# Encoder layer (HGRN2 and neighbourhood attention): keys and queries of the first attention half as seven block products in a stretch of their own

## The chip, the cores and the metric

The kernel runs on one core of one Trainium2 chip. The metric is the time of one execution on the device in microseconds (us), the median of several runs; lower is better. Five engines take part, each with its own instruction queue: PE (TensorE, matrix products), DVE (VectorE), ACT (ScalarE), POOL (GpSimd) and SP (SyncE, which only issues DMAs here). PE writes its results to PSUM banks; ACT and DVE move them from there to SBUF.

## What is computed

One layer over 2048 tokens (a grid of 32 rows by 64 columns) of width 1024, all in float32:

```python
h = layernorm(x) * (1 + scale) + shift          # scale, shift, gate from c @ ada_w
q_h, i_h, zf_fw, zf_bw, g_h, q_n, k_n, v_n, g_n = split(h @ w_in)   # 9 x 1024 columns
y_hg = hgrn2(q_h, i_h, zf_fw, zf_bw, g_h)       # gated linear recurrence, two directions, 8 heads
o_na = neighbourhood_attention(q_n, k_n, v_n, rpb)   # 16 heads of 64, 8 x 16 window of the grid
y = concat([y_hg, o_na * silu(g_n)]) @ w_out
out = layernorm(2**0.25 * x + gate * y) * ln_g + ln_b
```

## The kernel before

**Numbers.** A float32 matrix is multiplied as a sum of a rounded part (`hi`, type float32r) and the rest (`lo`): `hi*hi + hi*lo + lo*hi`, three matmuls for one product of a 128x128 block of weights with 128x512 of h (`proj_mm`, L278 to 282). A split of a 128x512 tile is one ACT copy (`hi`) and one DVE subtraction (`lo`).

**h.** h is kept transposed as tiles `hts[g, k, s]`: token group g (512 tokens each), feature block k (8 of 128), s = 0 for `hi` and 1 for `lo`. Only one half of the tokens (1024, two groups) is on chip at a time.

**Order of the whole.** PE's order is the program's; DVE, ACT, POOL and SP get theirs from a scheduler that orders instructions by readiness and priority, except where an instruction is `pinned` to its place in the program. The stages are: start-up (layer norm of the first half, h, and unit 0's projections); the first attention half; HGRN over 8 heads and two halves; the second attention half; the output projection. A "unit" is a pair of attention heads (128 columns of each of keys, queries and gate; values go by two units, 256 columns).

**Start-up** (`startup`). Besides unit 0's keys, queries and gate it multiplies values of units 0 and 1 (`vproj`) and, in one place, the first group of unit 1's keys (`fourth`, L1294 to 1313).

**First attention half** (`first_half`). Eight units of four tiles each (`natten_woven`): scores (4 matmuls, L1067 and L1074), bias addition and softmax on DVE and ACT (L1083 to L1093), transposes on PE (L1116), copies to SBUF (L1120, L1122), and one step later the sums with the values (L1138). While the tiles of unit u run, PE also works through a "dense" stream: `first_stream` of unit u+1, that is every second time a value block, and then keys, queries and gate, 2 groups x 8 k x 3 matmuls each (`NCOL0` gives the columns). The last unit runs beside the projections of the first HGRN head (`hgrn_dense`). `weave` hands out the dense work in equal shares, two for each tile (`yield` in `natten_woven`), with `KUS` = 0.68 us counted for three matmuls. Weights come through `Chunks`: a 128x512 tile is loaded by SP's queue, split, and freed; four tiles each of raw, `hi` and `lo`.

**Preparation of a unit** (`Prep`). `piece` is called as soon as a projection group is in SBUF: `k` copies the two heads' keys to `KA` and `KB` (L1002), moves each copy to the other 64 partitions by a DMA from SBUF to SBUF (L1003; SP's queue in the first half, POOL's in the second), and writes the rest to `KL` (L1004); `q` and `gate` are alike. What the second attention half will need again is stored to DRAM (`nq_d`, `nk_d`, `ng_d`). `table` loads the position bias for a tile; `v` loads value tiles from DRAM.

**Beside it.** `first_half` also carries the rest of the modulation's gate vector (`gate_load`, `gate_sum`), the bias tables' writing to DRAM (`bias_pair`), and the layer norm of the second half of the tokens, whose transposed h is stored to DRAM (`rows`, `stats`, `scale`, `piece`).

**Pools.** Tags that a stage shares with others go to common buffers (`SH`: "e" 8, "q" 4, "vt" 4, "gt" 2, "sg" 4, "bk" 4 tiles of 128x512); a stage's own tags stand in `NB0` and the like, and a mapping (`SM0`) says which of its names use the common ones. PSUM: 2 banks "pj" for dense work, and 2 each of "sc", "pt" and "po".

**Output projection.** It already takes two token tiles at a time as seven block products (`OutPair`, matmuls at L1672 to L1674), with sums of y made on DVE and splits on POOL (L1656).

Of the kernel before, what the change touches and what calls it, by code (L numbers as in the profile page):

```python
# [10 lines left out]
F32 = mybir.dt.float32  # L11
# [27 lines left out]
def body(ctx: ExitStack, tc: tile.TileContext, t):  # L39
# [38 lines left out]
    nq_d = [dram(f"nq{i}", (P, 512)) for i in range(NPAIR)]  # L78
    nk_d = [dram(f"nk{i}", (P, 768)) for i in range(NPAIR)]
# [670 lines left out]
    def load_bias(p, j, kind, pin=lambda x: x):  # L750
# [5 lines left out]
        elif kind == "top":  # L756
            dma(bf[0:64, 0:11 * 64], table_ap(tint[p], 22, jt, 4, 4, 11))
            dma(bf[64:128, 0:8 * 64], table_ap(tedge[p], 15, jt, 4, 4, 8))
# [114 lines left out]
    def first_srcs():  # L873

        r = [t["w_v"][0][:, i * 512:(i + 1) * 512] for i in range(4)]
        for u in range(1, 8):
            if u % 2 == 0:
                r += [t["w_v"][u // 2][:, i * 512:(i + 1) * 512] for i in range(4)]
            r += [t["w_in"][c // P + u][:, i * 512:(i + 1) * 512] for _, c in NCOL0 for i in range(2)]
        return r + [t["w_in"][c // P][:, i * 512:(i + 1) * 512] for _, c in HCOL for i in range(2)]  # L880

    def first_stream(st, feed):

        if st.p % 2 == 0:
            for _ in vproj(t["w_v"][st.p // 2], nv_d[st.p // 2], 0, feed):
                feed.tick()
                yield 2.9
        todo = []
        for n, c in NCOL0:
            his, los = feed.take(2)  # L890
            for g in range(2):
                if st.raws[n][g]:
                    todo = [(n, g)]
                    continue
                pz = ps("pj")
                for k in range(KT):
                    proj_mm(pz, his, los, g, k)
                    if k == KT - 1:
                        st.raws[n][g] = evac(pz)
                        todo = [(n, g)]  # L900
                    if g == 1 and k % 4 == 3:
                        feed.free()
                    feed.tick()
                    if k == 1 and todo:
                        st.piece(*todo.pop())
                    yield KUS
        st.piece(*todo.pop())
# [52 lines left out]
    class Prep:  # L960


        def __init__(self, p, half, raws):
            self.p, self.half, self.raws = p, half, raws
            self.first = half and p == 0
            self.keep = half and p in (0, 7)
            self.Q, self.V, self.sg, self.bias, self.bk = {}, {}, {}, {}, {}

        def fetch(self, name):
            store, n0, n1 = {"q": (nq_d, 0, 512), "g": (ng_d, 0, 512), "k0": (nk_d, 0, 512), "k1": (nk_d, 512, 768)}[name]  # L970
            raw = tl("bk")
            dma(raw[:, 0:n1 - n0], store[self.p][:, n0:n1])
            self.bk[name] = raw

# [1004 lines left out]
```

## Time and profile before

| | us |
|---|---|
| median of 3 runs | 2556.86 (2555.92 to 2558.54) |
| profiled execution | 2557.55 |
| its span, first to last instruction | 2555.7 |
| PE busy in the span | 2531.9 |
| DVE busy | 1807.0 |
| ACT busy | 1487.8 |
| POOL busy | 260.5 |
| start-up, until the first dense matmul of the first attention half | 91.9 |
| first attention half, to about | 517 |
| granted TensorE clock | 0.999 of full speed |

A matmul's busy time in the profile overlaps that of the next one, since they are pipelined; distances from start to start tell what one costs PE. "PEld" is the loading of a matmul's weights, which runs beside the matmul before.

### The profile page before, as it was taken

Reading aid. Unit: us, or ns where it says so; the run is one execution under the profiler, and the core shown is the slowest. Engines: PE = TensorE matmul, PEld = TensorE weight load, DVE = VectorE, ACT = ScalarE, POOL = GpSimd, SP = SyncE. Lnnn points to the kernel's source line nnn. Section 1 sums busy time; section 2 is a strip of 40 time slices with the busy share of each in tenths; the row PEclk is TensorE's granted clock in tenths of the full one; section 3 lists DMA queues with packets and bytes.
Section 4 is the critical chain, followed back from the end, with each engine's and each line's share of the span. In section 5 each row is a group of like instructions: output and inputs, shape, how many; then the busy total and the mean of one; then the engine's idle time right before and its main releaser. Section 6 shows DMA issues by size and latency. Waiting matters only on the chain.

```text
span 2555.7 us, 46330 instructions
## 1 busy us (share of the span) xinstructions
PE 2531.9 (99%) x17124; PEld 2142.6 (84%) x17124; DVE 1807.0 (71%) x4479; ACT 1487.8 (58%) x2968; POOL 260.5 (10%) x361
## 2 busy tenths in 40 slices
PE   8999999999999999999999999999999999999998
PEld 7888888888888888888888888999888888888887
DVE  7545545387877778868887887646777778867776
ACT  5533544376666666666666666545677768752331
POOL 0000000000000000000000000011122222224442
PEclk9999999999999999999999999999999999999999
DMA  7576454212122226222222222445566667664552
GB/s 297 144 210 156 143 173 148 94 51 71 67 75 71 71 71 224 99 79 85 62 70 82 85 83 83 134 117 150 129 136 145 140 140 167 178 207 132 162 168 99
DMA packets 227202, 319.55 MB, mean 125 GB/s; under 512 B 37159, under 2 KB 110503, under 8 KB 225831
## 3 DMA queue, kind: packets, MB, share of 16 engines
q1 hardware_dynamic: 210175, 278.51, 35.7%
q0 software_dynamic: 16800, 38.07, 6.4%
q8 instruction: 135, 2.21, 0.4%
q14 instruction: 92, 0.75, 0.1%
HBM read 233.90 MB, written 74.33 MB: 121 GB/s over the span
## 4 chain that ended last, share of the span: by engine, by line
PE 94%; DVE 3%; DMA 2%; ACT 1%; issue 1%; SPq 0%; POOL 0%; DVEq 0%; ACTq 0%; POOLq 0%
PE pj L282 53%; PE pj L295 7%; PE ps L1138 4%; PE ps L1674 3%; PE ps L1672 3%; PE ps L1673 3%; PE ps L1116 3%; PE ps L488 2%; PE ps L480 2%; PE ps L1067 2%; PE ps L555 1%; PE ps L1072 1%; PE ps L584 1%; PE ps L586 1%; PE ps L527 1%; PE ps L667 1%
## 5 line engine op out<-in xcount | busy, mean ns | idle before, releaser
L282 PE MATMUL pj<-h,wh 128*128 128x512 f32 x3984 | 1265.0, 399 | 0.2 <-ACT vt L303 0.2
L282 PEld LDWEIGHTS pj<-h,wh 128*128 128x128 f32 x3984 | 721.6, 188 | 148.7 <-issue 10.5
L282 PE MATMUL pj<-h,wl 128*128 128x512 f32 x1992 | 780.2, 392 | 0.0
L282 PEld LDWEIGHTS pj<-h,wl 128*128 128x128 f32 x1992 | 373.8, 188 | 81.8
L1088 ACT ACTIVATE pbuf<-pbuf,mx 128x480 f32<-128x480 f32 (+5 forms) x256 | 152.4, 596 | 90.5 <-DVE mx L1083 89.8
L295 PE MATMUL pj<-wh,h 128*128 128x256 f32 x1024 | 195.0, 285 | 0.3 <-ACT e L797 0.3
L1083 DVE CUSTOM_DVE_ANT_1 pbuf<-ps,bias 128x480 f32<-128x480 f32 (+5 forms) x256 | 129.1, 539 | 80.8 <-PE ps L1072 62.1
L295 PEld LDWEIGHTS pj<-wh,h 128*128 128x128 f32 x1024 | 162.9, 191 | 3.5 <-issue 0.9
L273 DVE TENSOR_TENSOR wl<-wr,wh 128x512 fp32r<-128x512 f32 x192 | 131.2, 684 | 44.2 <-ACT wh L272 43.9
L272 ACT ACTIVATE wh<-wr 128x512 fp32r<-128x512 f32 x192 | 120.2, 626 | 70.8 <-PE pj L282 64.3
L295 PE MATMUL pj<-wl,h 128*128 128x256 f32 x512 | 144.7, 283 | 0.0
L1122 ACT ACTIVATE pt<-ps 120x384 f32<-120x384 f32 (+3 forms) x128 | 65.2, 509 | 125.8 <-PE ps L1116 125.7
L1656 POOL TENSOR_TENSOR yl<-yr,yh 128x512 fp32r<-128x512 f32 (+1 forms) x80 | 109.6, 1380 | 147.0 <-ACT yh L1655 121.9
L1120 DVE COPY pt<-ps 120x384 f32<-120x384 f32 (+3 forms) x128 | 74.8, 584 | 63.1 <-PE ps L1116 62.1
L1116 PE MATMUL ps<-ident,pbuf 128*128 128x128 f32 (+2 forms) x832 | 112.6, 272 | 0.8 <-ACT Z L789 0.2
L1116 PEld LDWEIGHTS ps<-ident,pbuf 128*128 128x128 f32 (+2 forms) x832 | 96.6, 136 | 18.3 <-DVE pbuf L1093 1.9
L1655 ACT ACTIVATE yh<-yr 128x512 fp32r<-128x512 f32 (+1 forms) x80 | 47.9, 607 | 102.2 <-DMA yr<-yq 39.5
L474 DVE TENSOR_TENSOR de<-e,de 128x512 f32<-128x512 f32 x64 | 44.2, 691 | 88.2 <-ACT de L473 88.2
L797 ACT ACTIVATE e<-pj 128x512 f32<-128x512 f32 x96 | 57.3, 597 | 83.9 <-PE pj L282 75.9
L1093 DVE TENSOR_SCALAR pbuf<-pbuf,mx 128x480 f32<-128x480 f32 (+5 forms) x256 | 99.9, 411 | 3.3
L295 PEld LDWEIGHTS pj<-wl,h 128*128 128x128 f32 x512 | 97.9, 191 | 1.0
L849 DVE TENSOR_TENSOR wl<-wr,wh 128x512 fp32r<-128x512 f32 x68 | 46.8, 690 | 66.8 <-ACT wh L848 64.5
(361 smaller groups left out, 4897.8 us busy)
## 6 DMA issues: line engine op xcount, KB each, us to landing
wr<-in_w_in SPq DMA_DIRECT2D x276, 256.0 KB
yr<-yq SPq DMA_DIRECT2D x78, 256.0 KB
bias<-tint POOLq DMA_DIRECT2D x24, 480.0 KB, 7.9
x<-in_x SPq DMA_DIRECT2D x32, 256.0 KB
ada<-in_ada_m SPq DMA_DIRECT2D x8, 1024.0 KB
wr<-in_w_v SPq DMA_DIRECT2D x32, 256.0 KB
nv<-vt SPq DMA_DIRECT2D x32, 256.0 KB
hs<-s SPq DMA_DIRECT2D x32, 256.0 KB
```

What stands on the lines that cost most here:

```text
L272: act.activation(hi, raw, AF.Copy)
L273: dve.tensor_tensor(lo, raw, hi, op=ALU.subtract)
L282: pe.matmul(pz, a, b, start=(k == 0 and n == 0), stop=(k == KT - 1 and n == 2))
L295: pe.matmul(pzs[tp][:, i * 256:(i + 1) * 256], a, b, start=(k == 0 and n == 0 and i == 0), stop=(k == KT - 1 and n == 2), skip_group_check ...
L1083: return dve.tensor_tensor_reduce(s[:, 0:nk].rearrange("p (r c) -> p r c", c=kw), sc[:, 0:nk].rearrange("p (r c) -> p r c", c=kw), bt[:, 0 ...
L1088: act.activation(s[:, 0:nk], s[:, 0:nk], AF.Exp, scale=-1.0, bias=mx[:, 0:1], accum_out=mx[:, 1:2])
L1093: dve.tensor_scalar(s[:, 0:nk], s[:, 0:nk], mx[:, 2:3], 1.0, op0=ALU.mult, op1=ALU.mult)
L1116: pe.transpose(ptp[0:cw, c * P:(c + 1) * P], s[:, c * cw:(c + 1) * cw], ident)
L1138: pe.matmul(self.po[R][hs_, j * P:(j + 1) * P], v[:, hh * 64:hh * 64 + 64], pts[hh][0:n * KW[j], c * P:(c + 1) * P], start=(c == 0), stop= ...
L1656: pool.tensor_tensor(lo[:, c], src[:, c], hi[:, c], op=ALU.subtract)
L1672: pe.matmul(bank, yh[:, kk], wh, start=start, stop=False, skip_group_check=True)
L1673: pe.matmul(bank, yh[:, kk], wl, start=False, stop=False, skip_group_check=True)
```

## The change

Units 1 to 7 no longer get their keys and queries beside the attention. After the start-up comes a new stage (`dense_half`, its pool "sa"):

- First PE finishes unit 1's gate (group 1; group 0 is now what `fourth` multiplies in the start-up) and the values of units 2 and 3. Meanwhile `sum_piece` makes sums of h for four pieces: POOL adds `hi` and `lo` of four blocks of h, DVE forms S1 = 21 + 22, S2 = S1 - 11, S3 = 11 - 21 and S4 = 12 - S2 (block ab is token group a, feature half b), and each is split again and stays in SBUF, 32 tiles in all.
- Then each unit's keys and queries are one 2x2 block product in Strassen's form (`Pair`): two column blocks (keys, queries) by two token groups, the 1024 features as two halves. POOL makes differences T1 to T4 of the weights' blocks, seven products of 4 x 3 matmuls go to two PSUM banks, and ACT and DVE combine them on the way out. The results are stored to `nk_d` and `nq_d`, which now hold all 1024 tokens.
- `gate_load`, `gate_sum` and most of `bias_pair` move into this stage.

In the first attention half each unit then fetches keys and queries back from DRAM (`fetch_top`, at the first tile of the unit before it), and `k` and `q` run one and two tiles later, pinned. The dense work beside the attention is what is left: gates of units 2 to 7, values of units 4 to 7, and the first HGRN head's projections (`second_stream`), handed out evenly over all 66 shares after a first 16 us. Unit 0's own preparation moves from the start-up's end to the beginning of this stage. The key copies (L1003) and the "top" bias tables (L757, L758) go to POOL's DMA queue.

```diff
@@ load_bias @@
         elif kind == "top":
-            dma(bf[0:64, 0:11 * 64], table_ap(tint[p], 22, jt, 4, 4, 11))
-            dma(bf[64:128, 0:8 * 64], table_ap(tedge[p], 15, jt, 4, 4, 8))
+            nc.gpsimd.dma_start(bf[0:64, 0:11 * 64], table_ap(tint[p], 22, jt, 4, 4, 11))
+            nc.gpsimd.dma_start(bf[64:128, 0:8 * 64], table_ap(tedge[p], 15, jt, 4, 4, 8))
             pool.memset(bf[64:128, 8 * 64:11 * 64], BIG)
@@ streams @@
-    def first_stream(st, feed):
...
+    SECOND = (2, "v2", 3, 4, 5, "v3", 6, 7)
...
+    def gate_stream(st, feed, gs):
+
+        his, los = feed.take(2)
+        for g in gs:
+            pz = ps("pj")
+            for k in range(KT):
+                proj_mm(pz, his, los, g, k)
+                if k == KT - 1:
+                    st.raws["g"][g] = evac(pz)
+                    st.piece("g", g)
...
+    def second_stream(preps, feed):
+
+        for x in SECOND:
+            if x in ("v2", "v3"):
+                for _ in vproj(t["w_v"][int(x[1])], nv_d[int(x[1])], 0, feed):
+                    feed.tick()
+                    yield 2.9
+            else:
+                yield from gate_stream(preps[x], feed, (0, 1))
+        return (yield from hgrn_dense(0, 0, feed=feed))
@@ Prep @@
+        def fetch_top(self):
+            for n, g, store, n0, n1 in (("k", 0, nk_d, 0, 512), ("q", 0, nq_d, 0, 512), ("k", 1, nk_d, 512, 768)):
+                raw = tl("bk")
+                dma(raw[:, 0:n1 - n0], store[self.p][:, n0:n1])
+                self.raws[n][g] = raw
...
-                (pinned if self.first and i < 3 else lambda x: x)((nc.gpsimd.dma_start if self.half else dma)(z[y, o].bitcast(F32), z[x, o].bitcast(F32)))
+                (pinned if self.first and i < 3 else lambda x: x)(nc.gpsimd.dma_start(z[y, o].bitcast(F32), z[x, o].bitcast(F32)))
@@ first_next @@
-        return {0: [(st.v, 0)], 1: [(st.table, "top", 0), (st.v, 1)], 2: [(st.v, 2)], 3: [(st.table, "top", 1)]}
+        return {0: [(st.fetch_top,), (st.v, 0)], 1: [(st.table, "top", 0), (st.v, 1), (st.k, 0)], 2: [(st.v, 2), (st.k, 1), (st.q, 0)],
+                3: [(st.table, "top", 1)]}
@@ new functions @@
+    def sum_piece(k):
+
+        whole = {}
+        for name in ("21", "22", "11", "12"):
+            a = tl("whole")
+            pool.tensor_tensor(a, block_of(name, k, 0), block_of(name, k, 1), op=ALU.add)
+            whole[name] = a
+        for name, x, y, op in (("S1", "21", "22", ALU.add), ("S2", "S1", "11", ALU.subtract), ("S3", "11", "21", ALU.subtract), ("S4", "12", "S2", ALU.subtract)):
+            w = tl("part")
+            dve.tensor_tensor(w, whole[x], whole[y], op=op)
+            whole[name] = w
+            hi, lo = (tl(f"{name}_{k}_{s}", F32R) for s in range(2))
+            act.activation(hi, w, AF.Copy)
+            dve.tensor_tensor(lo, w, hi, op=ALU.subtract)
+            sums[name, k, 0], sums[name, k, 1] = hi, lo
...
+    class Pair:
+        ORDER = (("11", "B11"), ("S2", "T2"), ("12", "B21"), ("S3", "T3"), ("S1", "T1"), ("22", "T4"), ("S4", "B22"))
...
+        def product(self, j):
+            if j in (0, 4):
+                self.X = ps("sc")
+            if j in (1, 5):
+                self.Y = ps("po")
+            bank = self.Y if j in (1, 3, 5) else self.X
+            wh, wl = self.w.pop(j)
+            name = self.ORDER[j][0]
+            for k in range(4):
+                kk = slice(k * P, (k + 1) * P)
+                hh, hl = (block_of(name, k, s) for s in range(2))
+                for n, (a, b) in enumerate(((wh, hh), (wh, hl), (wl, hh))):
+                    pe.matmul(bank, a[:, kk], b, start=(j in (0, 1, 4, 5) and k == 0 and n == 0), stop=(k == 3 and n == 2), skip_group_check=True)
+            with tc.high_priority(offset=PRI):
+                if j == 0:
+                    self.p1 = tl("pu")
+                    act.activation(self.p1, bank, AF.Copy)
+                elif j in (1, 3):
+                    u = tl("pu")
+                    dve.tensor_tensor(u, bank, self.p1, op=ALU.add)
+                    self.u2, self.u3 = (u, None) if j == 1 else (self.u2, u)
...
+    def dense_half(preps, feed, first, second):
...
+        for i, _ in enumerate(ahead()):
+            if i in (0, 4, 8, 10):
+                sum_piece((0, 4, 8, 10).index(i))
...
+        for n, (pr, j) in enumerate(jobs):
+            if n + AHD < len(jobs):
+                jobs[n + AHD][0].prepare(jobs[n + AHD][1])
+            pr.product(j)
+            if j == 3 and n // 7 + 2 < len(pairs):
+                pairs[n // 7 + 2].load(n // 7 % 2)
...
@@ first_half @@
+        total, first = 6 * 2 * KT * KUS + 2 * VLEN + HTOT, 16.0
+        feed.load(WR + 4)
+        upto(first)
+        cum = 0
         for w in range(8):
             extra = {i: slots[4 * w + i] for i in range(4)}
-            if w < 7:
-                nxt = Prep(w + 1, 0, {n: [None, None] for n, _ in NCOL})
...
+            nxt = preps[w + 1] if w < 7 else None
+            for c in natten_woven(st, nxt, pipe, extra, w == 7):
+                cum += c
+                upto(first + (total - first) * cum / 66)
             st = nxt
```

Here `prepare` combines (on POOL) and splits the weights of a product two products ahead (`AHD` = 2).

## The prediction before the result was seen

> **What bounds the kernel now.** I read the page's busy times, then the chain that ended last, then what PE waited for, then the stretch that the change rewrites.
>
> ```profile
> span 2555.7 us, 46330 instructions
> ...
> PE 2531.9 (99%) x17124; PEld 2142.6 (84%) x17124; DVE 1807.0 (71%) x4479; ACT 1487.8 (58%) x2968; POOL 260.5 (10%) x361
> ...
> PEclk9999999999999999999999999999999999999999
> ...
> PE 94%; DVE 3%; DMA 2%; ACT 1%; issue 1%; SPq 0%; POOL 0%; DVEq 0%; ACTq 0%; POOLq 0%
> ...
> PE ps L148 <- DVE ada L143: 5.6, 1, 5.6
> PE ps L236 <- ACT x L229: 5.1, 2, 4.9
> PE ps L1067 <- DMA KA<-KA: 1.5, 1, 1.5
> PE ps L1674 <- POOL yl L1656: 0.5, 1, 0.5
> ```
>
> PE is busy for 99% at a full granted clock and holds 94% of the chain; its longest waits (the last four lines) are two in the start and two short ones near the end. So the time is the sum of the matmuls. A kernel like this gets faster by issuing fewer matmuls, and slower only when a change makes PE wait.
>
> The stretch concerned starts when the start-up ends (92 us) and lasts until the first attention half does (517 us). Its windows, beside those of the second attention half and of the output projection:
>
> ```profile
> 92.00:517.00 425.00, 424.97 (x2548) 358.71 (x2549) 203.79 (x557) 182.74 (x386) 6.93 (x24) 1.00 0.51 153
> ...
> 1872.90:2120.60 247.70, 247.11 (x1729) 206.44 (x1729) 192.27 (x594) 176.56 (x413) 57.77 (x100) 1.00 0.63 140
> ...
> 2380.00:2440.00 60.00, 60.00 (x267) 1.00 0.51 167
> ...
> L282 PE MATMUL pj<-h,wh 128*128 128x512 f32 x811 | 256.5, 397 | 0.2 <-ACT vt L303 0.2
> L282 PE MATMUL pj<-h,wl 128*128 128x512 f32 x405 | 158.2, 391 | 0.0
> ...
> L849 DVE TENSOR_TENSOR wl<-wr,wh 128x512 fp32r<-128x512 f32 x61 | 42.0, 690 | 60.8 <-ACT wh L848 58.4 <-DMA nk<-e 1.9 <-DMA wr<-in_w_in 0.3
> L848 ACT ACTIVATE wh<-wr 128x512 fp32r<-128x512 f32 x61 | 37.7, 624 | 22.6 <-PE pj L295 14.2 <-PE pj L282 8.4
> ...
> L797 ACT ACTIVATE e<-pj 128x512 f32<-128x512 f32 x41 | 24.5, 597 | 62.4 <-PE pj L282 62.3
> ...
> L175 DVE CUSTOM_DVE_ANT_0 x<-x,s,gsum 128x512 f32<-128x512 f32 x8 | 6.0, 751 | 0.2
> L175 DVE CUSTOM_DVE_ANT_0 x<-x,s,adab 128x512 f32<-128x512 f32 x8 | 6.0, 745 | 0.1
> ```
>
> In a window row the numbers after the length are PE, PEld, DVE, ACT, POOL (the third row has PE alone), then the granted clock, DMA share and GB/s. PE is full in all three; in the stretch DVE is busy for only 204 of 425 us, ACT for 183. The third column of a group row is the mean, which for matmuls overlaps the next one; the price of a matmul is therefore taken from the chain, where it is start to start:
>
> ```profile
> 127.08 8.83 PE pj L295 x72
> ...
> 384.91 6.82 PE pj L282 x30
> ...
> 393.75 7.07 PE pj L282 x30
> ```
>
> A 128x512 matmul costs 6.82/30 = 0.227 us, or 7.07/30 = 0.236 in a run that follows attention's small matmuls. A 128x256 one of the values costs 8.83/72 = 0.123 us.
>
> **The change, part by part.**
>
> *Seven products for eight.* A unit's keys and queries now take 2 (k, q) x 2 token groups x 8 x 3 = 96 matmuls of this size; as 7 block products of 4 x 3 they take 84. Seven units: 84 fewer. (The start-up's extra group is the gate's instead of the keys'; 24 matmuls either way.) 84 x 0.227 = **-19.1 us**; at 0.236 it would be -19.8. The third window shows that code of this kind loses nothing per matmul: there the output projection, already in seven products, starts a matmul every 60/267 = 0.225 us (those in flight at the edges are counted too).
>
> *Supply of the products.* A product lasts 12 x 0.227 = 2.72 us. It needs one ACT and one DVE split (0.624 and 0.690), and per unit of 19.1 us two ACT and five DVE evacuations (0.6 to 0.7 each) and four weight differences on POOL. ACT has 9 x 0.62 = 5.6 us of work per unit, DVE 12 x 0.69 = 8.3, POOL (below) 5.2. A bank is written again one product after it was read at the earliest, 2.72 us for a 0.7 us read. PE hides all of it: 0. Without that cover one late evacuation per unit would cost about 0.7 x 7 = 5 us. Weights and stores are 8 x 256 KB per 19.1 us, 110 GB/s, where the output projection's window moves 167: hidden.
>
> *Sums of h.* New: 16 adds on POOL, 32 two-operand instructions on DVE, 16 copies on ACT. The second product needs S2. Nearest rows are POOL's and DVE's in the output projection:
>
> ```profile
> L1656 POOL TENSOR_TENSOR yl<-yr,yh x78: 1000/1297/1743, 2283.6 to 2531.6; 128x512 fp32r<-128x512 f32 x63, 128x384 fp32r<-128x384 f32 x15
> ...
> L1650 DVE TENSOR_TENSOR yr<-yr,yr 128x384 f32<-128x384 f32 x8 | 8.2, 1019 | 2.2 <-POOL yl L1656 2.2
> ...
> L1646 DVE TENSOR_TENSOR yr<-yr,yr 128x384 f32<-128x384 f32 x8 | 4.8, 605 | 6.1 <-issue 5.4 <-DMA yr<-yq 0.6
> ...
> 2291.53 5.09 POOL L1656 TENSOR_TENSOR yl<-yr,yh 128x512 fp32r<-128x512 f32 x4 [6.24 <-ACT yh L1655]
> ...
> 2292.86 1.63 DVE L1650 TENSOR_TENSOR yr<-yr,yr 128x384 f32<-128x384 f32 x1 [2.02 <-POOL yl L1656]
> ```
>
> The same DVE shape takes 0.605 or 1.019 us on average, and 1.63 while POOL is inside four of its own: DVE and POOL held each other up. The Trainium skill ("SBUF — State Buffer", Who interferes with whom) says that a DVE instruction with two SBUF inputs and a GpSimd one that reads SBUF exclude each other for a whole instruction; the trace agrees (1.63 beside 0.605). By it the sums and the first T1, T2 run one after another.
>
> One after another they take (16 + 2) x 1.297 + 32 x 0.690 = 45.4 us; side by side 23. The time allowed: the start-up's last h piece is split at 88 us,
>
> ```profile
> 87.45 0.69 DVE L1254 TENSOR_TENSOR h<-sg,h 128x512 fp32r<-128x512 f32 x1
> ...
> 91.92 0.73 PE L282 MATMUL pj<-h,wh 128*128 128x512 f32 x2 [0.18 <-ACT vt L303]
> ```
>
> and the second product starts after the gate's 24 matmuls, 192 of the values and the first product, 91.9 + 5.4 + 23.6 + 2.7 = 123.6 us, its last quarter 2 us later: 37 us. The last four DVE instructions (2.8) may come later still, and the first adds can start before 88. So the wait lies between 0 and 45.4 - 37 = 8 us. I take **+2**, near the lower end, because the first piece's inputs but one are ready early.
>
> *Values without attention between.* The second half of a value block needs the two banks that its first half has just filled. Where values stand alone before:
>
> ```profile
> 1675.89 0.39 PE L295 MATMUL pj<-wh,h 128*128 128x256 f32 x1 [0.27 <-ACT e L797]
> ```
>
> 0.27 us there and 0.18 in the row at 91.92 us; for one block, with what follows it, **+0.5**.
>
> *Attention with less beside it.* What stays beside it is six units' gates (288 matmuls), 384 of the values and 240 of the first HGRN unit: 528 x 0.227 + 384 x 0.123 = 167 us. Attention and the h transposes themselves are the rest of today's stretch: 1216 (811 + 405) x 0.227 + 576 x 0.123 = 347, and 425 - 347 = 78 us. The new stage lasts 245 us for 32 tiles, 7.6 us a tile, instead of 13.3. DVE keeps 204 - 33 splits x 0.690 - 12 us of gate sums = 169 us, and about 5 of unit 0's that ran before 92: 174 of 245, 71%. ACT keeps 183 - 33 x 0.624 - 27 evacuations x 0.597 + 5 = 151, 62%. The second attention half runs at 192/248 = 78% and 71% with 5.2 us a tile (48 tiles in 247.7 us), and PE loses 0.6 us there. So the engines suffice. I take **+1.0** (0.6 doubled; bounds 0 and 2).
>
> *Queues.* Key copies and top tables leave SP's queue for POOL's, ten DMAs a unit, and a unit's last key copy is asked for one tile ahead of its first scores, 7.6 us (before, most of a unit's 50 us ahead). One case of one tile's lead stands in the second half, in unit 7:
>
> ```profile
> 2196.58 0.61 ACT L1002 ACTIVATE KA<-e 64x512 fp32r<-64x512 f32 x1
> ...
> 2197.60 0.53 POOL L1003 DMA_DIRECT2D KA<-KA  x1 [2.15 <-ACT KA L1002]
> ...
> 2203.33 0.40 PE L1067 MATMUL ps<-KA,Q 128*128 128x360 f32 x1 [1.48 <-DMA KA<-KA]
> ...
> DMA to landing us min/median/max: 2.0/6.4/10.8
> ```
>
> Copy, issue and landing took 2203.33 - 2196.58 = 6.75 us, and PE waited 1.48 of them, the longest wait after the start-up. With 7.6 us the median is hidden, barely; a late landing (10.8 is the longest) is not. Unit by unit 0 to 1.48, seven units: 0 to 10. I take 0.3 each, **+2**. The second table has the same lead, but DVE reads it, and the tile's transposes come another 7.6 us later, of which softmax takes about 3.6 (scores to last share):
>
> ```profile
> 105.64 0.43 PE L1074 MATMUL ps<-KL,q 64*128 64x352 f32 x2
> ...
> 108.84 0.40 DVE L1093 TENSOR_SCALAR pbuf<-pbuf,mx 128x352 f32<-128x352 f32 x1
> ```
>
> That leaves 4 us of slack: 0. SP gains three fetches of 256 KB a unit, a tile or more before ACT reads them, and loses the copies: 0. Unit 0's keys and tables start when the products end, behind 16 us of dense work (before, 10 x 0.68); two landings of 6.4 us fit: 0.
>
> **Sum:** -19.1 + 2 + 0.5 + 1 + 2 = -13.6 us. The profiled execution took 2557.55 us (span 2555.7 and 1.85 around it); the median is 2556.86, 0.7 lower. 2557.55 - 13.6 = 2544.0, for the median **2543**. What a measurement can tell from no change is about 0.2%, 5 us.
>
> **Rivals.**
>
> 1. *The sums hold PE up.* If DVE's order puts the values' splits behind sums that wait for POOL, PE waits in the value block too: the 8 us bound, and some 4 more where POOL takes its slowest 1.743 on 16 adds (7 us, half behind PE): -19.1 + 12 + 3.5 = -3.6, 2553. For: the 1.63 us above. Against: 29 us of PE's work that comes first. 12%, between 2548 and 2556.
>
> 2. *POOL's queue makes each unit's keys late (slower).* Its order is kept: a copy stands behind two table transfers and a memset that waits for DVE. If copy to landing takes 10.8 + 1.2 instead of 6.75, PE waits 12.0 - 7.6 = 4.4 us at each of seven first scores: 31, so 2557 - 15.6 + 31 = 2572; it decides from 7.6 + 15.6/7 = 9.8 us on. For: the wait shown above. Against: that median. The Trainium skill ("SBUF — State Buffer", two separate sides) says that DVE's two-port instructions keep GpSimd from writing DMA descriptors, which would lengthen them; no row here tells its share. The 6.4 us were measured beside a DVE at 78%. 10%, 2557 to 2575.
>
> 3. *The products don't give what they save.* A bank change every 12 matmuls instead of 24 could cost an edge of 0.1 to 0.25 us (7.07 - 6.82 is 0.25 a run): 49 x 0.1 to 49 x 0.25 = 5 to 12, 2548 to 2555. Against: the third window. 7%.
>
> **How the numbers follow.** The forecast (71%) spans 2536 (0.236 a matmul and no wait give 2557 - 19.8 = 2537; the runs shown scatter by 1) to 2548 (5 us more at sums or keys). The range reaches to 2554, with rival 3 and the lower part of rival 1; it leaves out some 13%. Faster by over 0.2% (under 2551.7): 71 + 5 of rival 3 + 6 of rival 1 = 82%; within: 10%, the rest of these and the edge of rival 2; slower: 8%.
>
> **What would show it.** PE's count falls by 84. Sums, products and attention together end 13 us earlier than the stretch does now, and nothing changes behind. Right: product starts 0.227 us apart, one PE wait before S2's product, short ones on KA at a unit's first scores. Wrong: PE waits on KA of several us in each unit (rival 2), DVE's sum lines at twice 0.69 with PE behind them (rival 1), or gaps at each product's first matmul (rival 3).

## The result, and the profile after

| | us | ratio to before (95% interval) |
|---|---|---|
| before, median | 2556.44 (2555.92 to 2558.54) | |
| after, median of 4 runs | 2583.5 (2582.5 to 2585.0) | 1.0105 (1.0087 to 1.0122) |
| after, span of the profiled execution | 2581.4 | |

The change makes the kernel 27 us slower; 13.6 us faster was forecast. The times of kernels are medians of fast runs; two of the five runs of stats_spread (below) were slow, at a mean granted clock of 0.85 and 0.65, and are left out. From the page of the profile after: span, PE's busy time, and the chain that ended last.

```profile
span 2581.4 us, 46541 instructions
...
PE 2529.1 (98%) x17040; PEld 2138.8 (83%) x17040; DVE 1883.8 (73%) x4567; ACT 1502.3 (58%) x2991; POOL 373.4 (14%) x485
...
PE 80%; DVE 3%; DMA 2%; issue 1%; ACT 1%; POOL 0%; DVEq 0%; POOLq 0%; SPq 0%; ACTq 0%
```

The 84 matmuls are gone (17040 for 17124), but PE's busy time falls by 2.8 us only, and the span is 52 us above it, where it was 24 before. So PE waits. (PE's share of the chain falls from 94% to 80%, but most of that is no waiting: the shares add up to only 87% here, because this chain can be followed back no further than 339 us.) The windows of the three new stages (values and sums; products; attention) show where; columns as in the prediction, the granted clock third from the end:

```profile
90.40:134.66 44.26, 33.08 (x220) 31.51 (x219) 36.22 (x35) 14.87 (x26) 24.82 (x15) 0.85 0.31 102
134.66:268.00 133.34, 133.34 (x591) 110.40 (x590) 73.08 (x119) 41.85 (x72) 35.09 (x30) 1.00 0.55 153
268.00:546.60 278.60, 260.48 (x1682) 215.98 (x1680) 171.08 (x495) 143.59 (x320) 55.13 (x106) 0.96 0.62 171
```

The products are as forecast: 588 matmuls (the window counts a few in flight at its edges) in 133.3 us, 0.227 each, PE full. The values take 44 us, of which PE works 33, and the attention 278.6 for a forecast of 245. What PE waited for in these stages, in us: total, times, longest.

```profile
PE pj L295 <- ACT e L797: 5.4, 2, 5.0
PE ps L1081 <- DVE mx L1097: 5.4, 2, 3.4
PE ps L236 <- DVE pt L1134: 5.2, 1, 5.2
PE pj L295 <- ACT vt L303: 5.1, 1, 5.1
PE ps L1081 <- issue: 3.3, 2, 2.0
PE ps L1081 <- DMA KB<-KB: 1.8, 4, 1.1
```

A few single waits of 1 to 5 us, then, not many small ones. (L1081 is the scores' matmul, L1067 before; L1097 the bias addition, L1134 a copy of the transposed shares, L1017 the key copy's DMA.) The two waits put down to "issue", 1.3 and 2.0 us at the first scores of units 0 and 1, are for key copies too; of the second, the copy's issue, its time to landing and the scores:

```profile
306.62 0.55 POOL L1017 DMA_DIRECT2D KA<-KA  x1 [0.72 <-ACT KA L1016]
...
KA<-KA POOLq DMA_DIRECT2D x1, 64.0 KB, 7.3
...
314.02 0.36 PE L1081 MATMUL ps<-KA,q 128*128 128x264 f32 x1 [2.00 <-issue]
```

306.6 + 7.3 is 313.9 us, 0.1 ahead of the scores. With the 1.8 us of the last row of the list, key copies account for 5.1 us.

**A wait is paid twice.** The windows of the first wait of 5 us and of what follows it:

```profile
97.90:103.20 5.30, 0.31 (x3) 0.10 (x1) 5.30 (x6) 2.92 (x6) 3.47 (x4) 0.81 0.17 49
103.20:108.00 4.80, 4.78 (x22) 4.78 (x23) 4.80 (x5) 0.78 (x2) 3.57 (x3) 0.50 0.29 82
```

After the wait PE is full again, but at a granted clock of 0.50: 22 matmuls in 4.8 us. The trace has seven such windows in the three stages, each of 3.41 or 6.83 us; a 128x512 matmul starts every 0.427 us in them instead of 0.227. Added up from PE's starts: the attention's stage lost 17.7 us in gaps of over 0.9 us and 11.8 to half clock (half of the 23.5 us worked in it); the values' stage 11.3 and 4.2. The Trainium skill ("TensorE: Matmul & The Clock Gate", Part 1) has windows of 3.4 us and half rate after an idle one; the 3.41 and the 0.427 us agree. It asks for a whole idle window; here less was enough. Waits of 2.0, 1.2 and 2.0 us (at 312.0, 418.7 and 449.0 us) were each followed by 3.41 us at half clock, while those of 1.3 and 1.1 us (at 285.0 and 511.2) were not. The second of them:

```profile
418.62:422.03 3.41, 1.98 (x9) 1.39 (x9) 2.10 (x7) 1.47 (x4) 1.37 (x3) 1.00 1.07 341
422.03:425.44 3.41, 3.41 (x12) 2.75 (x12) 0.58 (x3) 0.86 (x3) 0.61 (x1) 0.50 1.05 374
```

Cut into stretches of 3.413 us in step with these windows (from 40 us to the end), the traces of all the kernels here agree on this: a stretch at full clock in which PE was idle for 1.8 us or more was always followed by half clock, one with less than 1.1 us never, and in between both occur (1.43 us above was followed by it; 1.48 and 1.51 us in more_lead were not).

**The sums.** In the timeline, ahead of the end of that first wait:

```profile
99.83 5.01 POOL L1412 TENSOR_TENSOR sg<-h,h 128x512 f32<-128x512 f32 x3 [1.83 <-DVE q L1416]
100.28 1.75 DVE L1416 TENSOR_TENSOR q<-sg,q 128x512 f32<-128x512 f32 x1
101.94 1.75 DVE L1420 TENSOR_TENSOR S<-q,S 128x512 fp32r<-128x512 f32 x1
102.05 0.63 ACT L1419 ACTIVATE S<-q 128x512 fp32r<-128x512 f32 x1 [1.64 <-DVE q L1416]
102.59 0.58 ACT L797 ACTIVATE e<-pj 128x512 f32<-128x512 f32 x1
...
103.22 0.58 PE L295 MATMUL pj<-wh,h 128*128 128x256 f32 x1 [5.01 <-ACT e L797]
```

PE waits for a bank that ACT has to empty (L797). PE had filled that bank by 97.5 us (its last matmul there started at 97.11), but ACT's queue is in order, and ahead of the evacuation stand copies of the sums (L1419), which wait for DVE (L1416), which takes 1.75 us beside POOL's adds instead of 0.68 alone. The wait passes through three engines before it reaches PE.

**The attention.** Two of the waits in the timeline. First, DVE ahead of the scores that wait for their bank:

```profile
332.39 0.64 DVE L206 BATCH_NORM_STATS2 bnst<-x 128x6 f32<-128x512 f32 x1
...
333.49 0.68 DVE L206 BATCH_NORM_STATS2 bnst<-x 128x6 f32<-128x512 f32 x1
...
335.82 0.69 DVE L1002 TENSOR_TENSOR q<-bk,q 64x512 fp32r<-64x512 f32 x1
336.54 0.69 DVE L1003 TENSOR_TENSOR q<-bk,q 64x512 fp32r<-64x512 f32 x1
337.26 0.17 DVE L184 TENSOR_SCALAR v<-xmv 128x4 f32<-128x4 f32 x1
...
338.73 0.16 DVE L213 SCALAR_TENSOR_TENSOR xb<-xmv,xr 128x4 f32<-128x4 f32 x1
338.81 0.52 DVE L1097 CUSTOM_DVE_ANT_1 pbuf<-ps,bias 128x352 f32<-128x352 f32 x1
...
339.48 0.36 PE L1081 MATMUL ps<-KA,q 128*128 128x264 f32 x1 [3.41 <-DVE mx L1097]
```

The bias addition, which empties the bank, stands behind the later rows' statistics, a unit's key and query splits and the chain of the rates. Second, DVE's cast of a transposed h piece:

```profile
387.63 0.43 DVE L245 CAST s<-s 128x512 fp32r<-128x512 f32 x1 [8.25 <-DMA hs<-s]
...
389.48 0.43 DVE L1097 CUSTOM_DVE_ANT_1 pbuf<-ps,bias 128x264 f32<-128x264 f32 x1
...
391.06 0.55 DVE L1134 COPY pt<-ps 96x384 f32<-96x384 f32 x1
...
391.66 1.11 PE L236 MATMUL ps<-ident,x 128*128 128x128 f32 x4 [5.23 <-DVE pt L1134]
```

It stood 8.25 us for the store of the piece before, and the whole of DVE's queue behind it; a piece takes all three "s" buffers. The kernel before had a heavier chain and the same three buffers. It did all four rows of statistics in one tile, the 13th or the 24th of the 32; the changed kernel does two rows to a tile, from the 5th and the 18th on. From the kernel before:

```profile
250.54 1.28 DVE L206 BATCH_NORM_STATS2 bnst<-x 128x6 f32<-128x512 f32 x2
...
258.40 0.16 DVE L213 SCALAR_TENSOR_TENSOR xb<-xmv,xr 128x4 f32<-128x4 f32 x1
258.48 0.52 DVE L1083 CUSTOM_DVE_ANT_1 pbuf<-ps,bias 128x352 f32<-128x352 f32 x1
```

That bias addition came 8 us after the first of these statistics, and PE's only wait between 92 and 517 us was 0.2 us.

### The profile page after: what moved, and what is told of

Read it like the earlier page. It is cut to its first block, busy times and chain, and to the rows that moved or that the text cites. A ratio compares the mean times of both kernels' runs of the same rounds, so it can differ in the third digit from the quotient of the medians.

```text
span 2581.4 us, 46541 instructions
## 1 busy us (share of the span) xinstructions
PE 2529.1 (98%) x17040; PEld 2138.8 (83%) x17040; DVE 1883.8 (73%) x4567; ACT 1502.3 (58%) x2991; POOL 373.4 (14%) x485
## 4 chain that ended last, share of the span: by engine, by line
PE 80%; DVE 3%; DMA 2%; issue 1%; ACT 1%; POOL 0%; DVEq 0%; POOLq 0%; SPq 0%; ACTq 0%
PE pj L282 45%; PE pj L295 4%; PE ps L1839 3%; PE ps L1837 3%; PE ps L1838 3%; PE ps L1152 3%; PE ps L1130 3%; PE ps L488 2%; PE ps L480 2%; PE ps L1081 1%; PE ps L555 1%; PE ps L1086 1%; PE ps L584 1%; PE ps L586 1%; PE ps L527 1%
## 5 line engine op out<-in xcount | busy, mean ns | idle before, releaser
L282 PE MATMUL pj<-h,wh 128*128 128x512 f32 x3536 | 1130.1, 401 | 1.2 <-ACT vt L303 1.1
L282 PEld LDWEIGHTS pj<-h,wh 128*128 128x128 f32 x3536 | 640.0, 189 | 133.2 <-issue 10.1
L282 PE MATMUL pj<-h,wl 128*128 128x512 f32 x1768 | 695.0, 393 | 0.0
L282 PEld LDWEIGHTS pj<-h,wl 128*128 128x128 f32 x1768 | 333.0, 188 | 73.3
L295 PE MATMUL pj<-wh,h 128*128 128x256 f32 x1024 | 200.7, 289 | 10.8 <-ACT e L797 5.7
L1097 DVE CUSTOM_DVE_ANT_1 pbuf<-ps,bias 128x480 f32<-128x480 f32 (+5 forms) x256 | 129.2, 539 | 86.7 <-PE ps L1086 61.1
L273 DVE TENSOR_TENSOR wl<-wr,wh 128x512 fp32r<-128x512 f32 x192 | 131.4, 685 | 40.2 <-ACT wh L272 38.2
L474 DVE TENSOR_TENSOR de<-e,de 128x512 f32<-128x512 f32 x64 | 44.3, 691 | 87.8 <-ACT de L473 87.8
L1134 DVE COPY pt<-ps 120x384 f32<-120x384 f32 (+3 forms) x128 | 74.8, 584 | 34.2 <-PE ps L1130 33.4
L455 DVE TENSOR_TENSOR_SCAN c<-c,g 128x128 f32<-128x128 f32 x256 | 88.6, 406 | 7.4 <-ACT c L445 7.4
```

Source lines behind the costliest of these rows:

```text
L273: dve.tensor_tensor(lo, raw, hi, op=ALU.subtract)
L282: pe.matmul(pz, a, b, start=(k == 0 and n == 0), stop=(k == KT - 1 and n == 2))
L295: pe.matmul(pzs[tp][:, i * 256:(i + 1) * 256], a, b, start=(k == 0 and n == 0 and i == 0), stop=(k == KT - 1 and n == 2), skip_group_check ...
L455: dve.tensor_tensor_scan(c[:, sl], c[:, sl], L[:, sl], 0.0, op0=ALU.add, op1=ALU.subtract)
L1097: return dve.tensor_tensor_reduce(s[:, 0:nk].rearrange("p (r c) -> p r c", c=kw), sc[:, 0:nk].rearrange("p (r c) -> p r c", c=kw), bt[:, 0 ...
```

## The experiments

"Values" is the time from 90.4 us to the first product, "attention" from the last product to the last sum with the values; both by the profiled execution.

| kernel | median us | ratio to before (95% interval) | values us | attention us |
|---|---|---|---|---|
| after | 2583.5 | 1.0105 (1.0087 to 1.0122) | 44.3 | 278.6 |
| no_sums | 2569.0 | 1.0044 (1.0029 to 1.0059) | 29.9 | 277.5 |
| adds_on_dve | 2570.9 | 1.0053 (1.0038 to 1.0068) | 30.7 | 278.0 |
| keys_on_sp | 2598.3 | 1.0159 (1.0144 to 1.0175) | 44.6 | 290.3 |
| piece_two_buffers | 2585.8 | 1.0107 (1.0090 to 1.0123) | 43.5 | 281.5 |
| stats_spread | 2570.5 | 1.0045 (1.0027 to 1.0063) | 44.5 | 266.8 |
| rows_ahead | 2586.0 | 1.0111 (1.0097 to 1.0125) | 44.1 | 280.3 |
| keys_a_tile_earlier | 2582.3 | 1.0091 (1.0077 to 1.0105) | 44.9 | 276.2 |
| buffers_only | 2575.3 | 1.0071 (1.0055 to 1.0088) | 44.6 | 269.8 |
| thick_tiles | 2718.7 | 1.0632 (1.0611 to 1.0653) | 44.0 | 412.8 |
| all_four | 2553.4 | 0.9985 (0.9976 to 0.9994) | 29.2 | 267.2 |
| three_edits | 2549.8 | 0.9968 (0.9956 to 0.9980) | 29.5 | 259.4 |
| four_short_buffers | 2539.6 | 0.9930 (0.9916 to 0.9943) | 29.4 | 247.9 |
| more_lead | 2562.0 | 1.0019 (1.0010 to 1.0028) | 28.8 | 269.7 |
| more_lead_one_burst | 2563.2 | 1.0020 (1.0011 to 1.0029) | 29.2 | 272.7 |

### The sums

```diff
-        whole = {}
-        for name in ("21", "22", "11", "12"):
...
-            sums[name, k, 0], sums[name, k, 1] = hi, lo
+        for name, at in (("S1", "21"), ("S2", "11"), ("S3", "22"), ("S4", "12")):
+            for s in range(2):
+                sums[name, k, s] = block_of(at, k, s)
```

> The sums of h are left out (each of S1 to S4 is replaced by a plain block of h, so the products are formed from other data; the count of matmuls is the same). Theory A (the adds on POOL and the parts on DVE shut one another out, ACT's copies of the parts wait for DVE, and the evacuations of the value banks stand behind these copies in ACT's queue, so PE waits twice for 5 us and then runs at half its clock): the two PE waits in the stretch of the values go, the stretch falls from 44.3 us to about 30, and the whole from 2583.5 to 2567 to 2571. Rival (the stretch is slow because the values run alone with PE at once waiting for their loads): it stays above 40 us and the time above 2579. The attention's stage stays at 275 to 282 us by either.

14.5 us less, and the values' stage falls to 29.9 us: the sums carry what was lost there.

```diff
-            pool.tensor_tensor(a, block_of(name, k, 0), block_of(name, k, 1), op=ALU.add)
+            dve.tensor_tensor(a, block_of(name, k, 0), block_of(name, k, 1), op=ALU.add)
```

> The 16 adds of the sums go from POOL to DVE, nothing else. Theory A's part one (DVE and POOL shut one another out): the parts on DVE fall from 1.75 us each to about 0.7 and the adds from 1.7 to about 0.7, ACT's copies no longer wait long, the two PE waits of 5 us shrink below 1.5 us each, and the time falls to 2570 to 2575. Rival (what counts is only that the evacuation stands behind many copies on ACT, whatever DVE's pace): the waits stay above 4 us and the time above 2579.

12.6 us less, with all the sums made and DVE given more to do. The group rows between 90 and 135 us (busy, mean ns), first of the changed kernel, then of this one:

```profile
L1412 POOL TENSOR_TENSOR sg<-h,h 128x512 f32<-128x512 f32 x11 | 18.4, 1699 | 5.5 <-DVE q L1416 5.5
L1420 DVE TENSOR_TENSOR S<-q,S 128x512 fp32r<-128x512 f32 x15 | 16.3, 1113 | 0.0
```

```profile
L1420 DVE TENSOR_TENSOR S<-q,S 128x512 fp32r<-128x512 f32 x15 | 9.9, 685 | 0.0
...
L1412 DVE TENSOR_TENSOR sg<-h,h 128x512 f32<-128x512 f32 x11 | 8.4, 786 | 0.0
```

One engine alone does both in 18.3 us; the two side by side took 18.4 and 16.3. With the differences (L1416) DVE was busy for 32.4 us in this window beside POOL, and for 29.9 with the adds as well: POOL gave nothing. The Trainium skill ("SBUF — State Buffer", Who interferes with whom) has the two exclude each other, and this agrees (a subtraction takes 0.68 us alone and 1.75 beside an add). What the prediction's sum lacked is that a slower DVE holds back ACT's copies and through them PE.

### Queues and buffers

```diff
-                (pinned if self.first and i < 3 else lambda x: x)(nc.gpsimd.dma_start(z[y, o].bitcast(F32), z[x, o].bitcast(F32)))
+                (pinned if self.first and i < 3 else lambda x: x)((nc.gpsimd.dma_start if self.half else dma)(z[y, o].bitcast(F32), z[x, o].bitcast(F32)))
```

The two loads of the top tables likewise.

> In the first half of the attention the copies of the key rows between the partition halves and the loads of the top bias tables are issued by SP, as before the change, instead of POOL. Theory a (POOL's queue makes keys and tables late): most of the 30 us lost in the attention's stage come back, 2553 to 2563. Theory b (the delay is in the order on DVE and ACT, not in a transfer): 2578 to 2589, and the stage stays at 273 to 284 us; it may lose a little, as SP holds stores that wait for their data.

Neither: 15 us slower. PE's longest wait there:

```profile
PE ps L1081 <- DMA x<-in_x: 12.3, 2, 11.9
```

SP's queue is in order too, and holds the key copies among the loads of later rows of x: unit 1's second piece of keys, which ACT copied at 304.1 us, was issued there at 314.2 (305.8 and 306.6 in the kernel after). POOL's queue, the prediction's slower rival, was the better of the two.

```diff
-            h_piece(xs[g], k, a, b)
+            tmp = b.bitcast(F32)
+            act.activation(tmp, h_turn(xs[g], k), AF.Identity, scale=scale1[:, k:k + 1], bias=shift[:, k:k + 1])
+            dve.tensor_copy(a, tmp)
+            dve.tensor_tensor(b, tmp, a, op=ALU.subtract)
```

> In the pieces of h that the first half of the attention stores for later, the unsplit value lies in the buffer of the low part, so that a piece takes two of the three short buffers and not three. Theory c (DVE's cast waits 8.2 us for a store of the piece before, and the scores behind it hold PE for 5.5 us and then at half clock): the wait of DVE's casts for these stores falls from 12.5 us in all to under 4, the PE wait of 5.5 us goes, and the time falls by 6 to 10 us, to 2574 to 2578. Rival (PE waits there for something else that is late as well): the time stays within 3 us of 2583.5.

A miss: no gain, and the waits of DVE's casts for the stores came to 13.9 us. With three buffers in turn, a piece that takes two still writes where the piece before has a store under way.

### The attention's chains

```diff
-        for g, i in ((0, 3), (1, 16)):
+        for g, i in ((0, 3), (1, 17)):
             slots[i].append((rows, g))
-            slots[i + 1].append((stats, g, 0))
-            slots[i + 2].append((stats, g, 2))
-            slots[i + 3].append((scale, g, 0))
-            slots[i + 6].append((scale, g, 1))
+            for r in range(4):
+                slots[i + 1 + r].append((stats, g, r))
+            slots[i + 5].append((rates, g))
+            slots[i + 5].append((scale, g, 0))
+            slots[i + 8].append((scale, g, 1))
             for k in range(KT):
-                slots[i + 4 + k].append((piece, g, k))
+                slots[i + 6 + k].append((piece, g, k))
```

> The norm of the later rows of x is spread: one row's statistics in each tile of the attention, the rates in a tile of their own (before: two rows in each of two tiles, the rates right behind, and the splits of a unit's keys and queries in the same tile). Theory b (the bias additions stand in DVE's queue behind this chain, so that the scores wait for their bank): the PE waits at the ends of these chains (3.6 us in unit 1's tile 3, 2.1 us at unit 5's first tile) go, and with them two windows of half clock (6.83 and 3.41 us); the time falls by 7 to 12 us from 2583.5, to 2571 to 2577. Rival (DVE's work is the same, so the wait only moves to another tile): 2580 to 2587.

13.0 us less, a little more than theory b had; the two waits for the bias addition are gone, with the half clock behind them. As the diff shows, the pieces of h move two tiles later too, and the second group one tile more; DVE's longest wait for a store fell from 8.2 to 3.4 us. How much of the gain is the statistics alone was not tested.

```diff
-            slots[i].append((rows, g))
...
+                for r in range(4):
+                    slots[i - 5 + r].append((rows, g, 0, (r,)))
+                slots[i - 1].append((rows, g, 1, (0, 1)))
+                slots[i].append((rows, g, 1, (2, 3)))
```

> The second group's rows of x are loaded half by half: the first halves one row to a tile in the four tiles before, as their buffers come free, the second halves in two tiles. Theory c2 (the stores of h take 7 us because eight loads of 256 KB are issued in one burst beside a unit's keys and queries, and DVE's cast of the next piece waits for them): the wait of the cast falls from 8 us to under 3, the PE wait of 5.4 us in unit 3's tile 1 and a window of half clock of 6.83 us go, and the time falls by 6 to 9 us, to 2574 to 2578. Rival (three short buffers are too few at any rate): the wait stays and the time is within 3 us of 2583.5.

A miss: 2.5 us more, and a cast still stood 7.0 us for a store. The burst of loads was not the cause.

```diff
-        return {0: [(st.fetch_top,), (st.v, 0)], 1: [(st.table, "top", 0), (st.v, 1), (st.k, 0)], 2: [(st.v, 2), (st.k, 1), (st.q, 0)],
+        return {0: [(st.fetch_top,), (st.v, 0)], 1: [(st.k, 0), (st.k, 1), (st.table, "top", 0), (st.v, 1)], 2: [(st.v, 2), (st.q, 0)],
```

> The second piece of the next unit's keys is made one tile earlier, and both pieces ahead of the next bias table in POOL's queue. Theory a2 (POOL's queue itself is not slow, but these copies land 6 to 8 us after they could be issued, and the last of them starts only a tile ahead of its use): the PE waits of 3.2 us at unit 1's first tile and 1.9 us at unit 4's go, with two windows of half clock of 3.41 us; the time falls by 4 to 9 us, to 2575 to 2580. Rival (the table is what the scores wait for next, and it now comes later): no gain, 2582 to 2590.

1.2 us less, within the scatter of its runs (2577 to 2583). The wait at unit 1's first scores went; the one at unit 0's grew from 1.3 to 1.9 us and now had 6.83 us of half clock behind it, and the others stayed.

The edits of adds_on_dve, stats_spread, rows_ahead and keys_a_tile_earlier together:

> Adds of the sums on DVE, statistics spread, rows loaded ahead and keys a tile earlier, together. If each of these causes is a wait of its own, the gains add up: 12.6 us for the adds, and 20 to 28 us for the three of the attention's stage, 2543 to 2552, under the kernel before. If the waits only move from one to another, less than half of the second part comes back: 2558 to 2568. PE waits of more than 1.5 us in the attention's stage: at most one by the first, four or more by the second.

2553.4, 30 us less than after and just above the first range, with three PE waits of over 1.5 us: between the two theories. Waits of 2.7 and 4.4 us remained, both behind casts that waited for stores, and 2.3 us at unit 0's first scores, each with 6.83 us of half clock behind it.

All of these, a piece in two buffers (as piece_two_buffers), and room for a fourth:

```diff
-    NB0 = {"V": 6, "pbuf": 4, "pt": 4, "yv": 1, "bias": 3, "x": 8, "s": 3}
+    NB0 = {"V": 6, "pbuf": 4, "pt": 4, "yv": 1, "bias": 3, "x": 8, "s": 4}
...
-            b = tl("pbuf")
+            b = tl("pbuf", shape=None if half else [P, 384])
```

> As all_four, and each piece of h takes two of four short buffers instead of three of three (the attention's work buffers are 384 columns wide instead of 512, which makes the room). Theory c3 (with three buffers, either way, a piece always writes into a buffer whose store was issued one tile ago, and that store takes 7 to 8 us; with four it was issued two tiles ago): the waits of the casts for the stores fall from some 12 us to under 2, the PE waits of 3.0 and 4.8 us go with two windows of half clock of 6.83 us, and the time falls by 9 to 14 us from all_four, to 2540 to 2544. Rival (the stores stand on SP behind loads that wait, for longer than two tiles): less than 4 us, above 2549.

2539.6: 13.9 us less than all_four, 17.9 less than before. Its windows of the three stages:

```profile
90.40:119.80 29.40, 29.33 (x219) 27.79 (x218) 29.36 (x44) 14.58 (x26) 12.00 (x4) 1.00 0.46 152
119.80:253.00 133.20, 133.20 (x590) 110.30 (x589) 73.40 (x120) 41.75 (x71) 37.43 (x33) 1.00 0.55 154
253.00:500.90 247.90, 246.97 (x1682) 207.23 (x1680) 170.00 (x495) 142.76 (x320) 52.39 (x103) 1.00 0.68 192
```

The same 1682 matmuls of the attention's stage in 247.9 us instead of 278.6, with DVE as busy as before (170 us); the clock is full and no wait of PE is over 0.3 us.

The same buffers on the changed kernel, with nothing else of these edits:

> The changed kernel with only the short buffers changed as in four_short_buffers (two of four to a piece). If the store of h was a cause of its own: the wait of the cast (8.2 us) and the PE wait of 5.4 us go, with the half clock of 6.83 us behind it, 7 to 10 us less, 2573 to 2577. If the wait passes to another tile: within 3 us of 2583.5.

8.2 us less on the changed kernel alone, as expected. Two buffers to a piece help only if there are four.

Without the two edits that had given nothing by themselves:

> The adds on DVE, the statistics spread, two of four short buffers to a piece; the rows of x in one burst and the keys a tile later, as in the changed kernel. If three causes (sums, statistics, short buffers) carry the loss, as rows_ahead and keys_a_tile_earlier alone moved the time by +2.5 and -1.2 us: 2538 to 2544. If the keys cost as much as their PE waits show (3.2 us at unit 1's first tile with a window of half clock of 6.83 us behind it, 0.6 at unit 4's): 2545 to 2550, with the wait at unit 1's first tile in the profile.

2549.8: 10.2 us above four_short_buffers. The keys matter once the rest is mended. The wait, with the key copy ahead of it:

```profile
289.81 0.55 POOL L1017 DMA_DIRECT2D KA<-KA  x1 [0.73 <-ACT KA L1016]
...
KA<-KA POOLq DMA_DIRECT2D x1, 64.0 KB, 9.5
...
299.37 0.56 PE L1081 MATMUL ps<-KA,q 128*128 128x264 f32 x1 [4.16 <-issue]
```

The copy landed 9.5 us after its issue, at 299.3, and the scores started. The wait stands at unit 1's first scores, with 6.83 us of half clock behind it (3.4 us lost), and there are 0.6 and 0.8 us for key copies at units 4 and 7: 9 of the 10 us. So of the two edits left out it is the keys' that counts.

```diff
-        total, first = 6 * 2 * KT * KUS + 2 * VLEN + HTOT, 16.0
+        total, first = 6 * 2 * KT * KUS + 2 * VLEN + HTOT, 24.0
```

> As four_short_buffers, with 24 units of dense work instead of 16 ahead of the attention's first scores. The PE wait of 2.3 us at unit 0's first scores and the half clock of 6.83 us behind it (about 3.4 us) go: 4 to 6 us less than four_short_buffers, 2535 to 2540. Rival (the later units have less dense work beside them, and one of them waits instead): within 2 us.

A plain miss: 22.5 us slower. The wait at unit 0's first scores was gone already, and four others of over 2 us came, of which the longest reads in the timeline:

```profile
326.46 1.28 DVE L206 BATCH_NORM_STATS2 bnst<-x 128x6 f32<-128x512 f32 x2
...
329.80 1.29 DVE L206 BATCH_NORM_STATS2 bnst<-x 128x6 f32<-128x512 f32 x2
...
331.74 0.56 PE L1081 MATMUL ps<-KA,q 128*128 128x264 f32 x1 [6.31 <-DVE mx L1097]
```

On DVE, whose order the scheduler chose anew, the statistics and a unit's splits stand ahead of the bias addition again. That 8 us of lead make it choose so was read, not tested.

> As more_lead, but the second group's rows of x are loaded in one burst again. If the burst was a cause of the slow stores by itself, a wait of DVE's casts of over 3 us and a PE wait come back, 4 us or more above more_lead; if the buffers were all of it, within 2 us of more_lead.

Within 2 us of more_lead (1.2 above): the burst costs nothing that these runs can tell.

### Thin tiles or the order

```diff
-        for n, (a, b) in enumerate(((wh, hts[g, k, 0]), (wh, hts[g, k, 1]), (wl, hts[g, k, 0]))):
-            pe.matmul(pz, a, b, start=(k == 0 and n == 0), stop=(k == KT - 1 and n == 2))
+        for r in range(1 + twice[0]):
+            for n, (a, b) in enumerate(((wh, hts[g, k, 0]), (wh, hts[g, k, 1]), (wl, hts[g, k, 0]))):
+                pe.matmul(pz, a, b, start=(k == 0 and n == 0 and r == 0), stop=(k == KT - 1 and n == 2 and r == twice[0]))
...
```

> The changed kernel, in whose attention stage each matmul of the dense work (gates, values, the first HGRN unit; 528 of 128x512 and 384 of 128x256) is issued twice, so that these projections come out doubled; nothing else differs. The stage gets 528 x 0.227 + 384 x 0.123 = 167 us more of PE's work and a tile 13 us instead of 8. If the tiles were too thin for the chains behind one another (statistics, stores, key copies), the waits go with the half clock behind them: 29 us less, 2717 to 2727 in all, and PE waits under 4 us in sum in the stage. If the order of the instructions makes the waits whatever the thickness, they stay: 2742 to 2752, and over 12 us of PE waits.

2718.7, and in the attention's stage:

```profile
267.60:680.40 412.80, 411.84 (x2594) 352.25 (x2592) 174.41 (x495) 145.08 (x320) 54.73 (x107) 1.00 0.41 116
```

912 matmuls more, and only 134 us more than after; 167 were added, so 33 came back. The longest PE wait was 0.6 us, the clock full, the chains, buffers and queues those of the changed kernel. The values' stage, ahead of it, lost its 15 us as in the kernel after. So it was the thin tile that laid the waits bare, and not the order by itself. A longer tile also thins every load (the DMA share falls from 0.62 to 0.41), so this run doesn't tell a chain's length from a load that is too high; four_short_buffers does, where the tile stays at 7.7 us, DVE at 170 us and the DMA share at 0.68, and the waits are gone.

## Why the prediction was wrong, point by point

**Right: the products.** -19.1 us, their supply at nothing, no cost at a change of banks (rival 3). 588 matmuls took 133.2 to 133.3 us.

**Right: the frame.** With its waits mended (four_short_buffers) the change comes near what the prediction's parts give: values 29.4 us where 5.4 + 23.6 + 0.5 were forecast, attention 247.9 where 245 + 1 + 2 were, and 17.9 us less than before in all.

**Wrong: "Attention with less beside it", +1.0 (bounds 0 and 2); over 20 us measured.** The stage took 278.6 us, 30.7 more than in four_short_buffers; some 7 to 10 of these belong to the key copies ("Queues", below). This is the main failure. The step compared busy shares (DVE at 71%; its work, 171 us, was as forecast) with those of the second attention half and said "the engines suffice". They do, on average. But PE's order is fixed, the scores of a tile need a bank that DVE empties, and DVE works in order. A chain of 8 us on DVE cost PE nothing in a tile of 13.3 us, and the chains of the two groups cost it 3.4 and 2.0 us in one of 8 us. Throughput was counted, latency per tile was not. Two causes showed: statistics and rates ahead of bias additions (13.0 us by stats_spread, which moves the pieces of h too) and three short buffers (8.2 alone, 13.9 with the rest mended), both of them because tiles were thin (thick_tiles).

**Wrong: "Sums of h", +2 (0 to 8); 14.9 measured** (44.3 less 29.4). The exclusion was named, with the right rows, and rival 1 described the course nearly as it went, on ACT's copies and evacuations instead of DVE's splits. The size was wrong: the sum asked when S2 is needed, where PE did not wait at all, and priced DVE at 0.690 and POOL at 1.297 us; side by side they took about 1.75 and 1.70.

**Missing: the half clock.** No step priced it; it took about 16 us of the 45 lost (11.8 and 4.2), about half as much as the waits themselves (17.7 and 11.3).

**Right in kind, too small: "Queues", +2 (0 to 10); 7 to 10 read from the trace.** The waits on key copies at a unit's first scores came as described: 5.1 us, or 6.3 with the 1.2 us at unit 4's (put down to DVE, but a copy landed 0.13 us before its end), and 1.7 or 3.4 us for the half clock behind them. Unit 0's keys, priced at 0, cost 1.3 of these. By edits the keys cost 1.2 us alone and 10.2 with the rest mended. Rival 2, the slower one, asked for 12 us from copy to landing; the copies landed 3.3 to 8.3 us after issue, so it got the side right without its condition. That POOL's queue was chosen was no loss: moving copies and tables back to SP cost 15 us.

The chance of slower, 8%, was put on rival 2 alone. The waits that came were each unlikely to be named, but there were many in-order queues whose cover the change thinned, and no rival stood for them together.

## What to carry to other kernels

When work is moved out from beside a latency-bound stage, look at its longest chain per tile on each in-order queue (statistics, casts behind stores, key copies) and compare it with the new length of a tile; busy shares don't show it. Before giving POOL a share of two-operand adds whose other half is on DVE in the same stretch, measure DVE alone: here it was as quick as both. Count a PE wait of about 2 us or more as the wait and the half clock behind it (1.7 or 3.4 us lost here; after waits of 2.7 us and more it always came, after 1.2 to 2.4 us more often than not), and mend such waits together: single mends gave at most 13 us, all of them together 44.

## What the runs showed of the hardware

PE's granted clock fell to half for 3.41 or 6.83 us in the changed kernel (13.65 in keys_on_sp, around a wait of 11.9 us), and not only after a whole idle window: PE idle for 1.8 us of a stretch of 3.413 us was always enough, under 1.1 us never. In four_short_buffers, without such gaps, the clock stayed full from the start-up to the end. A DVE subtraction of 128x512 takes 0.68 us alone and 1.75 beside POOL's add, and the add 1.70 there, against 0.79 on DVE. A key copy of 64 or 128 KB from SBUF to SBUF by POOL's queue landed 3.3 to 8.3 us after its issue in the changed kernel, and up to 9.6 us in three_edits.
